# Latent branch: query and key projections as one product of 352 columns, two token blocks at a time, over halves of the rows

## The chip, the cores and the metric

The kernel runs on one core of one Trainium2 chip. The metric is device time of one execution in microseconds (us). The kernel before took 1448.16 us, the median of three runs (1447.72 to 1449.43). A core has a matrix engine (TensorE, PE in the profile), a vector engine (VectorE, DVE), a scalar engine for activations and copies (ScalarE, ACT), a general one (GpSimd, POOL) and a queue that issues transfers (SyncE, SP). Matrix products are written to PSUM, eight banks of 512 fp32 numbers on each of 128 partitions; everything else lives in SBUF.

## The reference

Two layers work on 256 latent tokens (`x`) and 256 context tokens (`ctx`), 1024 channels wide. A layer normalises and modulates the tokens to `h`, projects `h` through `w_in` to the queries, keys and values of four attention branches, gates and merges the branches, and ends with a gated MLP. In layer 1 the context tokens only serve as keys and values: no queries of theirs are needed. The branch that is changed is the fourth, the latent one (MLA):

```python
q = (rms_norm(qa, qa_g) @ w_qb)        # qa: 192 columns of h @ w_in
kv = (rms_norm(kva, kva_g) @ w_kvb)    # kva: 128 columns of h @ w_in
k_rope = rms_norm(kr, ...)             # kr: 32 columns of h @ w_in, shared by the 4 heads
```

Queries and keys get a rotary part of 32 numbers per head (latent tokens only), 4 heads attend over all 512 tokens (context queries over context alone).

## The kernel before

Every large product is made in three matmuls (`mm3`, lines 277 to 280): both factors are split into a high part in the fast fp32 format and a low rest, and high x high, high x low and low x high are added up. The tokens' split halves `hh` and `hl` stay in SBUF, 8 chunks of 128 channels by 512 tokens. A weight tile is loaded and split by `wload` (line 267): one transfer on SP's queue into `raw`, a cast on ACT into `wh` (line 272), a subtraction on DVE into `wl` (line 257, a helper). `raw`, `wh` and `wl` have four slots each, of up to 1024 columns.

`win_block` (line 442) makes one block of columns of `h @ w_in`. It loads two weight tiles (512 rows each) and walks over token halves j (256 tokens) and token blocks a (128 tokens): 8 row chunks times `mm3`, with the tokens as the stationary factor and the weights streaming. Both blocks of a half land in one PSUM buffer of the pool `acc_p` (three buffers, line 243), and a function `use` then takes them out: one copy on ACT, the norm, and a list of later steps. Those wait in the list `later`; `due` runs one of them at each turn of the generator, and `flush` (line 438) runs what is left, one a turn.

For the latent branch there are two such blocks: `mkv` (160 columns: 128 of the key and value rank, 32 rotary; both halves in either layer) with `use_mkv` (line 709), and `mqa` (192 columns; the halves `qh`, both in layer 0 and the first alone in layer 1) with `use_mqa` (line 748). Each leaves five steps per half: a transposition of the normalised rank (`put`), for either token block the second product with `w_kvb` or `w_qb` into an `acc` buffer with its norm and rotary work (`tok`, lines 725 and 764, products at lines 728 and 768), and for either the transposition of the heads into `kT` or `qT` (`mla_T`, line 741).

Several generators are interleaved by `drive` (line 282): each has a weight, and the one whose count of turns divided by its weight is smallest goes next. The drive at lines 1034 to 1037 holds the attention of the third branch (`attend`, weight `na` = 10 per token half), `merge(1, ...)` (line 933, weight 8, one turn per 128 output channels), the chain of the two latent blocks and `flush` (weight 22 in layer 0, 10.64 in layer 1), and in layer 0 four turns of modulation work. A turn of `merge` loads a gate tile, makes the gate product (24 matmuls) into one `acc` buffer, a tanh on ACT (line 943) reads it, makes the branch product (6 matmuls) into another, and a DVE instruction (line 949 or 951, shown under its helper's line 254) reads that. It keeps a branch tile for four turns. The next drive (line 1039) attends over the latent branch and runs `merge(2, ...)`.

The order of this program is the first wish: the kernel is built with `schedule_with_timeline_sim=True`, so a planner that simulates the engines at compile time fixes each engine's order and gives out buffers, and may put a later instruction ahead of one that waits. In the trace the matmuls of different generators do stand mixed.

Of the kernel before, what the change touches and what calls it, by code (L numbers as in the profile page):

```python
# [31 lines left out]
def _r(a, n):  # L32
    return np.arange(a, a + n)
# [4 lines left out]
    "naq": _r(NAQ, 256),  # L38
    "dk": _r(DK, 256), "dv": _r(DV, 256), "dq": _r(DQ, 256),
    "gkv": np.concatenate([_r(GK, 128), _r(GV, 128)]), "gq": GQ_PERM,  # L40
    "mkv": np.concatenate([_r(MKVA, 128), _r(MKR, 32)]), "mqa": _r(MQA, 192),
}
GBR_PERM = np.concatenate([_r(0, 64), _r(128, 64), _r(64, 64), _r(192, 64)])
MOD_GROUPS = [(1, 0), (2, 4), (3, 5)]
FGRP = [(0, 8), (8, 8), (16, 6)]
# [2 lines left out]
def tile_keys():  # L48
    ks = []
    for g in range(3):  # L50
        ks += [("mod", g, kt, half) for kt in range(KD) for half in range(2)]
    ks += [("nakv", t) for t in range(4)]
    ks += [("win", blk, t) for blk in BLOCKS for t in range(2)]
    ks += [("gate", i, m) for i in range(4) for m in range(KD)]
    ks += [("br", i, h) for i in range(4) for h in range(2)]
    ks += [("out", m) for m in range(KD)]
    ks += [("up", f) for f in range(2 * NF)]
    ks += [("down", g, m) for g in range(len(FGRP)) for m in range(KD)]
    ks += [("qb",), ("kvb",)]
    return ks  # L60
# [7 lines left out]
def _kp(w):  # L68

    k, n = w.shape  # L70
    return w.reshape(k // P, P, n).transpose(1, 0, 2).reshape(P, -1)


def host_tile(key, l, w):
    k = key[0]
    if k == "mod":
        _, g, kt, half = key
        if g == 0 and l == 0:
            o = w["w_mod"][0].reshape(2, 4, P, 6, KD, P)[half, :, :, 0:2, kt]
            return o.transpose(1, 0, 2, 3).reshape(P, 1024)  # L80
        c = MOD_GROUPS[g][half] * KD + kt
        return w["w_mod"][l, :, c * P:(c + 1) * P].T
    if k == "nakv":
        return _kp(w["w_in"][l, key[1] * 256:(key[1] + 1) * 256, NAK:NAK + 512])
    if k == "win":
        _, blk, t = key
        return _kp(w["w_in"][l, t * 512:(t + 1) * 512][:, BLOCKS[blk]])
    if k == "gate":
        return _kp(w["w_gate"][l, key[1], :, key[2] * P:(key[2] + 1) * P])
    if k == "br":  # L90
        wb = w["w_branch"][l, key[1]]
        if key[1] == 2:
            wb = wb[GBR_PERM]
        return _kp(wb[:, key[2] * 512:(key[2] + 1) * 512])
    if k == "out":
        return _kp(w["w_out"][l, :, key[1] * P:(key[1] + 1) * P])
    if k == "up":
        return _kp(w["w_up"][l, :, key[1] * P:(key[1] + 1) * P])
    if k == "down":
        f0, n = FGRP[key[1]]  # L100
        return _kp(w["w_down"][l, f0 * P:(f0 + n) * P, key[2] * P:(key[2] + 1) * P])
    if k == "qb":
        a = w["w_mla_qb"][l].reshape(2, 96, 384).transpose(1, 0, 2).reshape(96, 768)
        o = np.zeros((P, 768), a.dtype)
        o[:96] = a
        return o
    if k == "kvb":
        return w["w_mla_kvb"][l]
# [123 lines left out]
def backbone(ctx: ExitStack, tc, wb, xT, cc, cb, sm, rg, bias, cst, out):  # L232
# [209 lines left out]
    def win_block(l, blk, halves, use):  # L442
# [3 lines left out]
        for j in halves:  # L446
# [9 lines left out]
            due(0)  # L456
            yield

    def head_rstd(*parts):

        v = tiny.tile([P, 16], F32, name="v")
        o = 0
        for ap, mul, add in parts:
            a, h, d = ap.shape[1:]
            sq = tmp.tile([P, T], F32, name="t")
            sv = sq[:, :a * h * d].rearrange("p (a h d) -> p a h d", a=a, h=h)
            A.activation(out=sv, in_=ap, func=AF.Square)
            vo = v[:, o:o + a * h]
            V.tensor_reduce(out=vo, in_=sq[:, :a * h * d].rearrange("p (h d) -> p h d", d=d), op=ALU.add, axis=AX.X)
            V.tensor_scalar(out=vo, in0=vo, scalar1=mul, scalar2=add, op0=ALU.mult, op1=ALU.add)  # L470
            o += a * h
        return pow_mhalf(v[:, :o], o)
# [9 lines left out]
    for l in range(L):  # L482
# [225 lines left out]

        def use_mkv(t0, na, ps):
            st = stage()  # L710
            A.copy(st[:, :, 0:160], ps[:, :, 0:160])
            a, krn = st[:, :, 0:128], st[:, :, 128:160]
            r = head_rstd((a.unsqueeze(2), 1.0 / 128, EPS), (krn.unsqueeze(2), 1.0 / 32, EPS))
            tt(V, a, a, r[:, 0:2].unsqueeze(2).to_broadcast([P, 2, 128]), ALU.mult)
            tt(V, krn, krn, r[:, 2:4].unsqueeze(2).to_broadcast([P, 2, 32]), ALU.mult)
            if t0 < 2:
                rope(st[:, :, 160:192].unsqueeze(2), krn.unsqueeze(2), 1, 2, t0)
                krn = st[:, :, 160:192]
            got = {}

            def put():
                got["ma"] = mw["ka"]
                to_T(got["ma"].unsqueeze(1), st[:, :, 0:128], vec("kvag"), A)

            def tok(t):
                ma = got["ma"]
                kv = acc_p.tile([P, 512], F32, name="acc")
                mm(kv, lhsT=ma[:, t * P:(t + 1) * P], rhs=mw["kv"], start=True, stop=True)  # L728
                kv4 = kv.rearrange("p (h d) -> p h d", h=4)
                A.copy(Vt["ml"][:, t0 + t].rearrange("p (h d) -> p h d", h=4), kv4[:, :, 64:128])  # L730
                skv = stage().rearrange("p a n -> p (a n)")[:, :384].rearrange("p (h d) -> p h d", h=4)
                kn = skv[:, :, 0:64]
                A.copy(kn, kv4[:, :, 0:64])
                r = head_rstd((kn.unsqueeze(1), 1.0 / 64, EPS))
                tt(V, kn, kn, r.unsqueeze(2).to_broadcast([P, 4, 64]), ALU.mult)
                G.tensor_copy(skv[:, :, 64:96], krn[:, t].unsqueeze(1).to_broadcast([P, 4, 32]))
                got[t] = lambda: mla_T(kT, skv, t0 + t, vec("mkc" if t0 else "mkx", 0, 96), A)

            return [put, lambda: tok(0), lambda: tok(1), lambda: got[0](), lambda: got[1]()]
# [7 lines left out]

        def use_mqa(t0, na, ps):
            st = stage()
            A.copy(st[:, :, 0:192], ps[:, :, 0:192])  # L750
            r = head_rstd((st[:, :, 0:192].unsqueeze(2), 1.0 / 192, EPS))
            tt(V, st[:, :, 0:192], st[:, :, 0:192], r.unsqueeze(2).to_broadcast([P, 2, 192]), ALU.mult)
            got = {}

            def put():
                tp = tp_p.tile([P, 4, P], F32, name="tp")
                for i in range(2):
                    for a in range(2):
                        nc.tensor.transpose(tp[:96, 2 * i + a], st[:, a, 96 * i:96 * i + 96], ident)
                got["ma"] = mw["qa"]  # L760
                for i in range(2):
                    A.mul(got["ma"][:96, i], tp[:96, 2 * i:2 * i + 2].rearrange("p a t -> p (a t)"), vec("qag", i, 96))

            def tok(t):
                ma = got["ma"]
                qps = acc_p.tile([P, 512], F32, name="acc")
                for i in range(2):
                    mm(qps[:, :384], lhsT=ma[:96, i, t * P:(t + 1) * P], rhs=mw["q"][:96, i], start=i == 0, stop=i == 1)  # L768
                sq_ = stage().rearrange("p a n -> p (a n)")
                A.copy(sq_[:, :384], qps[:, :384])  # L770
                sqv = sq_[:, :384].rearrange("p (h d) -> p h d", h=4)
                q4 = sqv
                r = head_rstd((q4[:, :, 0:64].unsqueeze(1), 1.5, 96 * EPS), (q4[:, :, 64:96].unsqueeze(1), 3.0, 96 * EPS))
                tt(V, sqv[:, :, 0:64], q4[:, :, 0:64], r[:, 0:4].unsqueeze(2).to_broadcast([P, 4, 64]), ALU.mult)
                rr = r[:, 4:8].unsqueeze(2).to_broadcast([P, 4, 32])
                if t0 < 2:
                    qr = sq_[:, 384:512].rearrange("p (h d) -> p h d", h=4)
                    tt(V, qr, q4[:, :, 64:96], rr, ALU.mult)
                    rope(sqv[:, :, 64:96].unsqueeze(1), qr.unsqueeze(1), 0, 2, t0 + t)
                else:  # L780
                    tt(V, sqv[:, :, 64:96], q4[:, :, 64:96], rr, ALU.mult)
                got[t] = lambda: mla_T(qT, sqv, t0 + t, vec("mqc" if t0 else "mqx", 0, 96), V)

            return [put, lambda: tok(0), lambda: tok(1), lambda: got[0](), lambda: got[1]()]
# [222 lines left out]
        for t in range(4):  # L1007
# [25 lines left out]
        O = newO()  # L1033
        drive((attend([(0, 2), (1, 3)], probs_gq, Vt["gq"], lambda h: 64 * (h // 2), post_plain(O)), na),
              (merge(1, O1), 8),
              (chain(win_block(l, "mkv", A2, use_mkv), win_block(l, "mqa", qh, use_mqa), flush()), (16 + nq) * (1, 0.56)[l]),
              *early(4))
        O1 = newO()
        drive((attend(PAIR, probs_ml, Vt["ml"], lambda h: 64 * h, post_plain(O1)), na), (merge(2, O), 8 * (1, 1.96)[l]),
# [187 lines left out]
```

## Time and profile before

| | |
|---|---|
| median of three runs | 1448.16 us |
| profiled execution: its time | 1449.59 us |
| profiled execution: span from first to last instruction | 1447.8 us |
| mean granted TensorE clock | 0.992 of full speed |
| matmuls | 8562 |
| bytes moved by transfers | 202.20 MB |

The profile is of one execution. Busy time of an engine counts its instructions from start to end, and matmuls overlap one another, so for PE the distance from the start of a matmul to the start of the next says what it costs. The chain of waits goes back from the last instruction, at each step to what released it. In layer 0 the matmuls of the two latent blocks run between 250 and 324 us of the span, in layer 1 between 1068 and 1125 us.

### The profile page before, as it was taken

To read this page: it belongs to the slowest core of one execution; us is meant where nothing else is said; L and a number is where in the kernel's file an instruction comes from. 1 tells how busy PE (TensorE), PEld (TensorE's weight loads), DVE (VectorE), ACT (ScalarE), POOL (GpSimd) and SP (SyncE) were. 2 spreads that over 40 slices of the span, in tenths; PEclk is the share of its full clock that TensorE was granted. 3 is DMA by queue.
4 is the path that set the end of the run, shared out by engine and by line. 5 is a ranking of instruction groups with operands and counts; after the bars stand their busy time and mean duration, and the time that the engine had idled before them with its cause. 6 is when DMAs were issued, how large, how long until landed. Compare 5 with 4: busy or idle time off the path is not lost.

```text
span 1447.8 us, 22404 instructions
## 1 busy us (share of the span) xinstructions
PE 1406.1 (97%) x8562; PEld 1194.4 (82%) x8562; DVE 1057.1 (73%) x1976; ACT 656.6 (45%) x1201; POOL 148.4 (10%) x143
## 2 busy tenths in 40 slices
PE   6899999999999999999999999999999999899998
PEld 3687778776777889888888888898898889799998
DVE  5578777657676656999999654777876676686884
ACT  5344555443333334533234432455655554564662
POOL 0243102112100000000000000053122300000000
PEclk9999999999999999999999999999999999899999
DMA  9433032223234441565797222242232334455553
GB/s 376 172 102 95 31 105 79 90 63 128 88 116 161 140 166 45 182 196 177 237 323 238 101 99 84 88 138 89 83 127 96 119 129 133 152 182 185 180 185 107
DMA packets 57931, 202.20 MB, mean 140 GB/s; under 512 B 6560, under 2 KB 8096, under 8 KB 57184
## 3 DMA queue, kind: packets, MB, share of 16 engines
q1 hardware_dynamic: 57824, 200.77, 41.6%
q8 instruction: 68, 1.11, 0.3%
q14 instruction: 39, 0.32, 0.1%
HBM read 199.69 MB, written 1.05 MB: 139 GB/s over the span
## 4 chain that ended last, share of the span: by engine, by line
PE 87%; issue 7%; DVE 3%; ACT 2%; POOL 1%; DMA 1%; SPq 0%; POOLq 0%; DVEq 0%; ACTq 0%
PE acc L278 25%; PE acc L279 24%; PE acc L280 24%; PE av L876 3%; PE sc L792 2%; PE tp L868 2%; DVE wl L257 1%; PE tp L647 1%; PE tp L372 1%; ACT wh L272 1%; PE sc L804 1%; DMA mraw<-in_wb_dram 1%; PE acc L768 1%; PE acc L728 1%; POOL st L257 0%
## 5 line engine op out<-in xcount | busy, mean ns | idle before, releaser
L272 ACT CAST wh<-raw 128x1024 fp32r<-128x1024 f32 (+1 forms) x272 | 279.7, 1029 | 463.3 <-PE acc L279 384.0
L278 PE MATMUL acc<-hh,wh 128*128 128x256 f32 (+1 forms) x1248 | 422.4, 340 | 6.2 <-ACT hh L424 3.9
L257 DVE TENSOR_TENSOR wl<-raw,wh 128x1024 fp32r<-128x1024 f32 (+1 forms) x272 | 326.8, 1202 | 137.1 <-ACT wh L272 135.9
L280 PE MATMUL acc<-hh,wl 128*128 128x256 f32 (+1 forms) x1248 | 419.3, 336 | 0.0
L279 PE MATMUL acc<-hl,wh 128*128 128x256 f32 (+1 forms) x1248 | 418.2, 336 | 0.0
L278 PEld LDWEIGHTS acc<-hh,wh 128*128 128x128 f32 x1248 | 238.5, 192 | 35.1 <-ACT hh L424 4.4
L280 PEld LDWEIGHTS acc<-hh,wl 128*128 128x128 f32 x1248 | 239.0, 192 | 25.1 <-issue 2.8
L279 PEld LDWEIGHTS acc<-hl,wh 128*128 128x128 f32 x1248 | 239.2, 192 | 24.8 <-issue 2.7
L350 DVE SCALAR_TENSOR_TENSOR junk<-raw,cact 128x1024 bf16<-128x1024 f32 x128 | 157.1, 1227 | 17.4 <-DMA raw<-in_wb_dram 17.0
L278 PE MATMUL acc<-wh,hh 128*128 128x256 f32 (+3 forms) x496 | 149.4, 301 | 5.8 <-ACT hh L424 5.8
L257 POOL TENSOR_TENSOR r<-v,mhalf 128x4 f32<-128x4 f32 (+3 forms) x59 | 80.0, 1359 | 701.6 <-DVE v L405 365.1
L279 PE MATMUL acc<-wl,hh 128*128 128x256 f32 (+3 forms) x496 | 147.5, 297 | 0.0
L280 PE MATMUL acc<-wh,hl 128*128 128x256 f32 (+3 forms) x496 | 145.3, 298 | 1.1 <-DVE hl L254 1.1
L279 PE MATMUL acc<-al,wh 128*128 128x256 f32 (+1 forms) x370 | 121.6, 329 | 0.0
L280 PE MATMUL acc<-ah,wl 128*128 128x256 f32 (+1 forms) x370 | 121.6, 329 | 0.0
L278 PE MATMUL acc<-ah,wh 128*128 128x256 f32 (+1 forms) x370 | 121.5, 328 | 0.0
L254 DVE SCALAR_TENSOR_TENSOR u<-acc,smt,u 128x255 f32<-128x255 f32 (+1 forms) x184 | 108.9, 594 | 1.5 <-ACT u L1126 0.4
L278 PEld LDWEIGHTS acc<-wh,hh 128*128 128x128 f32 x496 | 95.4, 192 | 14.6 <-ACT hh L424 8.3
L818 ACT ACTIVATE p<-sc,nm 128x512 f32<-128x512 f32 (+1 forms) x120 | 74.3, 620 | 70.3 <-DVE nm L815 35.2
L280 PEld LDWEIGHTS acc<-wh,hl 128*128 128x128 f32 x496 | 94.9, 192 | 8.9 <-issue 3.4
L279 PEld LDWEIGHTS acc<-wl,hh 128*128 128x128 f32 x496 | 95.5, 193 | 6.7 <-issue 4.2
L815 DVE TENSOR_REDUCE nm<-sc 128x1 f32<-128x512 f32 (+1 forms) x120 | 70.4, 595 | 17.1 <-PE sc L804 7.9
(173 smaller groups left out, 2016.0 us busy)
## 6 DMA issues: line engine op xcount, KB each, us to landing
raw<-in_wb_dram SPq DMA_DIRECT2D x328, 512.0 KB, 3.5
mraw<-in_wb_dram SPq DMA_DIRECT2D x16, 512.0 KB, 10.2
raw<-in_wb_dram SPq DMA_DIRECT2D x20, 384.0 KB, 2.9
x<-in_xT_dram SPq DMA_DIRECT2D x2, 1024.0 KB, 6.3
bt<-in_bias_dram SPq DMA_DIRECT2D x8, 256.0 KB, 2.7
xt<-in_xT_dram SPq DMA_DIRECT2D x2, 1024.0 KB, 8.5
raw<-in_wb_dram SPq DMA_DIRECT2D x4, 320.0 KB, 2.9
cact<-in_cb_dram SPq DMA_DIRECT2D x1, 1024.0 KB, 11.4
```

Of the source, the lines that this page charges most:

```text
L254: return V.scalar_tensor_tensor(out=out, in0=in0, scalar=scalar, in1=in1, op0=op0, op1=op1)
L257: e.tensor_tensor(out=out, in0=a, in1=b, op=op)
L272: A.copy(h[:, :w], r[:, :w])
L278: mm(ps, lhsT=a[0], rhs=b[0], start=first, stop=False)
L279: mm(ps, lhsT=a[0], rhs=b[1], start=False, stop=False)
L280: mm(ps, lhsT=a[1], rhs=b[0], start=False, stop=last)
L350: V.scalar_tensor_tensor(out=junk, in0=r, scalar=1.0, in1=cact[:, st_], op0=ALU.mult, op1=ALU.mult, accum_out=o)
L792: mm(sps[:, :n], lhsT=q[o:o + d, c:c + P], rhs=k[o:o + d, T - n:], start=True, stop=True)
L815: V.tensor_reduce(out=nm, in_=sps[:, :n], op=ALU.max, axis=AX.X, negate=True)
L818: A.activation(out=p[:, :n], in_=sps[:, :n], func=AF.Exp, bias=nm, accum_out=s)
L868: nc.tensor.transpose(tp[:, i], p[:, i * P:(i + 1) * P], ident)
L876: mm(av[64 * j:64 * j + 64], lhsT=V_[:, 4 - nk + i, vcol(hd):vcol(hd) + 64], rhs=PTs[j][:, i], start=i == 0, stop=i == nk - 1, tile_positi ...
```

## The change

A new generator `win_mla` takes the place of the two `win_block`s in the chain. Key and query columns lie side by side in new weight tiles (`("mla", t)`, four per layer, 256 rows by 352 columns). For a half of the tokens it opens two `acc` buffers, one per token block, loads the two tiles of one half of the rows, runs both token blocks over these 4 row chunks, then the other half of the rows. The second half of the tokens begins with the half of the rows that is still loaded, and loads the first one again: six loads a layer in place of four. Where a half needs no queries (layer 1, context), the matmuls take only the first 160 columns. Then both `use` functions run on the two buffers, with one copy per token block, and their ten steps go to `later`, keys first. The weight of the chain in `drive` stays as it was.

```diff
-    "mkv": np.concatenate([_r(MKVA, 128), _r(MKR, 32)]), "mqa": _r(MQA, 192),
 }
+MLA_COLS = np.concatenate([_r(MKVA, 128), _r(MKR, 32), _r(MQA, 192)])
...
+    ks += [("mla", t) for t in range(4)]
...
+    if k == "mla":
+        return _kp(w["w_in"][l, key[1] * 256:(key[1] + 1) * 256][:, MLA_COLS])
...
+    def win_mla(l, halves, use_kv, use_q):
+        n = len(MLA_COLS)
+        for j in range(2):
+            nn = n if j in halves else 160
+            pss = [acc_p.tile([P, T], F32, name="acc") for _ in range(2)]
+            for step, i in enumerate(((0, 1), (1, 0))[j]):
+                if j == 0 or step:
+                    w = [wload(l, ("mla", 2 * i + t), 2, n) for t in range(2)]
+                for a in range(2):
+                    t = 2 * j + a
+                    for kt in range(4):
+                        mm3(pss[a][:, :nn], tuple(z[:, 4 * i + kt, t * P:(t + 1) * P] for z in (hh, hl)),
+                            tuple(z[:, kt % 2, :nn] for z in w[kt // 2]), step == 0 and kt == 0, step == 1 and kt == 3)
+                    due(0)
+                    yield
+            steps = use_kv(2 * j, 2, pss)
+            if j in halves:
+                steps = steps + use_q(2 * j, 2, pss)
+            later.extend([f, 0] for f in steps)
+            due(0)
+            yield
...
         def use_mkv(t0, na, ps):
             st = stage()
-            A.copy(st[:, :, 0:160], ps[:, :, 0:160])
+            for i in range(2):
+                A.copy(st[:, i, 0:160], ps[i][:, 0:160])
...
         def use_mqa(t0, na, ps):
             st = stage()
-            A.copy(st[:, :, 0:192], ps[:, :, 0:192])
+            for i in range(2):
+                A.copy(st[:, i, 0:192], ps[i][:, 160:352])
...
-              (chain(win_block(l, "mkv", A2, use_mkv), win_block(l, "mqa", qh, use_mqa), flush()), (16 + nq) * (1, 0.56)[l]),
+              (chain(win_mla(l, qh, use_mkv, use_mqa), flush()), (16 + nq) * (1, 0.56)[l]),
```

## Rows read from the trace of the kernel before

**Rows 1.** The page: busy time, share of the span and instructions of each engine.

```profile
PE 1406.1 (97%) x8562; PEld 1194.4 (82%) x8562; DVE 1057.1 (73%) x1976; ACT 656.6 (45%) x1201; POOL 148.4 (10%) x143
```

**Rows 2.** The page: busy tenths and granted clock in 40 slices.

```profile
PE   6899999999999999999999999999999999899998
PEclk9999999999999999999999999999999999899999
```

**Rows 3.** The page: the chain of waits, by engine and by line.

```profile
PE 87%; issue 7%; DVE 3%; ACT 2%; POOL 1%; DMA 1%; SPq 0%; POOLq 0%; DVEq 0%; ACTq 0%
PE acc L278 25%; PE acc L279 24%; PE acc L280 24%; PE av L876 3%; PE sc L792 2%; PE tp L868 2%; DVE wl L257 1%; PE tp L647 1%; PE tp L372 1%; ACT wh L272 1%; PE sc L804 1%; DMA mraw<-in_wb_dram 1%; PE acc L768 1%; PE acc L728 1%; POOL st L257 0%
```

**Rows 4.** Windows: stretch, its length, busy us (instructions) per engine, clock, DMA.

```profile
250.00:346.00 96.00, 94.85 (x521) 71.50 (x520) 64.60 (x145) 43.31 (x104) 13.45 (x18) 1.00 0.29 93
1068.00:1146.00 78.00, 76.00 (x554) 64.19 (x553) 50.88 (x108) 43.54 (x92) 17.95 (x21) 1.00 0.34 112
```

**Rows 5.** Groups by line and shape: PE, one of three matmuls of either block.

```profile
L280 PE MATMUL acc<-wh,hl 128*128 128x160 f32 x64 | 17.7, 276 | 0.0
L280 PE MATMUL acc<-wh,hl 128*128 128x192 f32 x48 | 13.2, 274 | 0.0
```

**Rows 6.** Timeline of PE (start, duration): first and last of unbroken stretches.

```profile
269.71 0.28 PE L279 MATMUL acc<-wl,hh 128*128 128x160 f32 x1
...
274.85 0.27 PE L280 MATMUL acc<-wh,hl 128*128 128x160 f32 x1
...
303.94 0.27 PE L279 MATMUL acc<-wl,hh 128*128 128x192 f32 x1
...
306.40 0.28 PE L280 MATMUL acc<-wh,hl 128*128 128x192 f32 x1
...
1088.29 0.28 PE L278 MATMUL acc<-hh,wh 128*128 128x256 f32 x1
...
1090.68 0.28 PE L280 MATMUL acc<-hh,wl 128*128 128x256 f32 x1
...
282.44 0.40 PE L279 MATMUL acc<-hl,wh 128*128 128x512 f32 x1
...
287.49 0.39 PE L280 MATMUL acc<-hh,wl 128*128 128x512 f32 x1
```

**Rows 7.** Groups by line and shape: splitting a 768-column weight tile.

```profile
L272 ACT CAST wh<-raw 128x768 fp32r<-128x768 f32 x20 | 16.7, 835 | 46.7 <-PE acc L279 44.4 <-PE acc L280 2.3
L257 DVE TENSOR_TENSOR wl<-raw,wh 128x768 fp32r<-128x768 f32 x20 | 19.0, 952 | 2.3 <-ACT wh L272 2.3
```

**Rows 8.** Timeline of ACT, DVE, PE in layer 0: handover to the query tiles.

```profile
273.82 0.83 ACT L272 CAST wh<-raw 128x768 fp32r<-128x768 f32 x1 [1.76 <-PE acc L280]
275.16 0.83 ACT L272 CAST wh<-raw 128x768 fp32r<-128x768 f32 x1 [0.51 <-PE acc L280]
...
275.18 0.95 DVE L257 TENSOR_TENSOR wl<-raw,wh 128x768 fp32r<-128x768 f32 x1
...
276.85 0.94 DVE L257 TENSOR_TENSOR wl<-raw,wh 128x768 fp32r<-128x768 f32 x1
...
276.68 0.49 PE L278 MATMUL acc<-Oh,wh 128*128 128x512 f32 x1
277.23 0.44 PE L603 MATMUL tp<-C,st 128*128 128x128 f32 x2
277.91 0.70 PE L792 MATMUL sc<-kA,qA 64*128 64x256 f32 x2 [0.24 <-ACT p L818]
```

**Rows 9.** Timeline of PE, ACT, DVE: readers of a gate and branch product.

```profile
288.88 0.40 PE L280 MATMUL acc<-Oh,wl 128*128 128x512 f32 x1
...
288.64 0.59 ACT L943 ACTIVATE t<-acc 128x512 f32<-128x512 f32 x1
...
289.91 0.68 DVE L254 SCALAR_TENSOR_TENSOR t<-t,acc 128x512 f32<-128x512 f32 x1
```

**Rows 10.** Timeline of PE, layer 1: query product behind its operand's copy.

```profile
1141.39 1.56 PE L768 MATMUL acc<-kB 96*128 96x384 f32 x4 [0.84 <-ACT kB L762]
```

## The prediction, before the changed kernel was run

> **What bounds the kernel now.** First the share of the span that each engine is busy: TensorE (PE) 97%, with VectorE (DVE) and ScalarE (ACT) far below it [rows 1]. Busy matmuls overlap, so this alone does not prove a bound. Second the slices of the span: PE stands at 9 almost throughout, and so does the granted clock, that is, its 2.4 GHz level [rows 2]. Third the chain of waits: PE holds 87% of it, and the three matmul lines of `mm3` hold 74% [rows 3]. Fourth the two stretches in which the changed blocks run, about 250 to 346 us in layer 0 and 1068 to 1146 us in layer 1: PE is busy 94.85 of 96 us and 76.00 of 78 us at clock 1.00, DVE 64.60 and 50.88, ACT 43.31 and 43.54, POOL 13.45 and 17.95 [rows 4]. So matmul time that goes here should come off the span, provided that PE still finds its next matmul ready.
>
> **1. The matmuls.** `win_block` multiplies every block of 128 tokens by 160 key columns and, on its own, by 192 query columns: 8 chunks of rows by 3 matmuls each. Layer 0 has 4 token blocks for either, 96 + 96 matmuls; layer 1 needs queries for 2 blocks, 96 + 48. The trace has 192 matmuls of 160 columns and 144 of 192 (one of three equal groups for each is shown, x64 and x48) [rows 5]. What counts is the distance from start to start, since a mean duration overlaps the next one. Over 47 unbroken matmuls of 160 columns it is (274.85 - 269.71) / 46 = 0.112 us; over 23 of 192 columns, (306.40 - 303.94) / 22 = 0.112; over 21 of 256, (1090.68 - 1088.29) / 20 = 0.1195; over 23 of 512, (287.49 - 282.44) / 22 = 0.2295 [rows 6]. The narrow ones cost alike: 160 and 192 columns lie on a floor, so two separate narrow products pay for it twice. No matmul of 352 columns of this kind is in the trace; its bounds are the rows of 256 and 512. Between these a column costs (0.2295 - 0.1195) / 256 = 0.00043 us, so I take 0.1195 + 96 x 0.00043 = 0.161 us.
>
> Layer 0: 192 x 0.112 = 21.5 us go, 96 x 0.161 = 15.5 come: -6.0. Layer 1: 144 x 0.112 = 16.1 go; 48 x 0.161 + 48 x 0.112 (the second half keeps 160 columns) = 13.1 come: -3.0. Sum **-9.0 us**. With 0.1195 for the new matmul it would be -15.0, with 0.2295 it would be +0.8.
>
> A rule speaks against this. The Trainium skill, page "TensorE: Matmul & The Clock Gate", section "Back-to-back issue gap", gives for the isolated gap of a warm matmul N/2.4 + 2.5 ns. By it 160, 192 and 352 columns are estimated at 69, 82 and 149 ns, and all the change would save about 0.4 us, since the columns in total do not change. The trace does not agree for the narrow ones: 0.112 us for both of them. The same section says that in a stream of weight loads and matmuls both set the spacing, which fits the floor.
>
> **2. The weight tiles.** Before, a layer loads 4 tiles here (2 of 640 columns, 2 of 768); after, 6 of 704, since the first half of the rows is loaded again for the second pair of token blocks. Each load costs a cast on ACT and a subtraction on DVE; the nearest, of 768 columns, take 0.835 and 0.952 us [rows 7]. Two more per layer are 1.7 us on ACT and 1.9 on DVE, in stretches where ACT has 53 and 34 us to spare and DVE 31 and 27 [rows 4]: they are hidden by PE's own work. SP gets two more transfers per layer in its order ahead of later gate weights; the DMA engines are busy 0.29 and 0.34 of these stretches [rows 4], so I cost that at nothing; if the cover goes, what is late is the next gate weight.
>
> What isn't free is the handover from one pair of tiles to the next. Four slots hold split weights; merge keeps two (its branch tile and a gate tile), so the next pair can be cast only when the old pair is done. In layer 0 the pair for the queries is cast from 273.82 on and ready at 277.79; in that time PE did other work, with gaps: a 512-column matmul at 276.68 was followed only 0.55 us later (0.32 more than its 0.23), the two transposes after it by the scores 0.68 later with 0.24 of idleness [rows 8]; that is 0.6 us lost, which I round up to 1.0 for what a row does not show. I count 0 for layer 1's handover, whose PE rows show no such gap, so half a microsecond on average. Each layer has one handover more than before: +1.0 for both layers if each of the four new ones costs 0.5 and the two old ones go. Bounds: 0, and 4 x 4 = 16 if none of the 4 us were covered.
>
> **3. The accumulators.** Three PSUM buffers are shared by the projections, merge (one for the gate product, one for the branch product, in turn) and the steps that follow on keys and queries. Before, a projection held one and left two. After, it holds two from the first matmul of a pass to the copies behind its last, so everybody else has one, for the 10 turns of `win_mla` in its chain: with the steps that `flush` has left, the chain has 10 + 14 = 24 turns in layer 0 (12 + 10 = 22 before) and 10 + 9 = 19 in layer 1 (9 + 8 = 17 before). With one buffer merge can't begin the branch product until the gate product has been read, nor the next gate product until the branch product has been. How late that is: a gate product's last matmul starts at 287.49 and ends about 0.39 us later, [rows 6]; its tanh ends at 289.23, because a cast stands ahead of it on ACT: 1.4 us. The branch product's last matmul ends at 289.28, its reader on DVE at 290.59: 1.3 us [rows 9]. About 2.7 us per step of merge, in which PE must have something else. If the turns run as the weights of `drive` say, 8 x 10/24 = 3.3 steps of merge fall into the passes in layer 0 and 8 x 10/10.64 = 7.5 in layer 1: 11 x 2.7 = 29 us to be covered. To cover it there are the 28.6 us of the projection's own matmuls (15.5 + 13.1), which need no new buffer, the scores, transposes and value products, and whatever later work the planned order pulls forward. I take 7% uncovered, **+2 us**; bounds 0 and +29. Queued behind a waiting gate matmul on PE is everything that PE does, so an uncovered wait goes straight to the span.
>
> **4. Copies and order.** One copy out of PSUM for two token blocks becomes two. ACT pays some 0.3 us more per pass, of its spare time. The steps on the first half's queries, with their rotary work on POOL, now come ahead of the second half's keys, and POOL is busy for 14 and 23% of the two stretches [rows 4]: nothing. Layer 1's last steps are then those of keys without rotary work in place of queries; the 0.84 us that PE waits there for the copy of the normalised queries [rows 10] may go or be replaced by a wait for the keys' copy. I count 0, bounds -1 and +2.
>
> **Sum.** -9.0 + 1.0 + 2.0 = -6.0 us on the profiled execution. That one took 1449.6 us, 1.8 more than its span, and 1.4 more than the median of the runs, 1448.16. So 1448.2 - 6.0 = **1442.2 us**.
>
> **The rivals.**
> *Accumulator starvation (slower).* The one buffer left decides once more than (9.0 - 1.0) / 29 = 28% of the merge waits have no cover. For it: layer 1, where passes fill nearly the whole stage and a step of merge has only 30 x 0.1195 = 3.6 us of matmuls against 2.7 us of waits. Against: matmuls of several generators already stand mixed in PE's order, and 47 matmuls of the key block ran in one go from 269.71 to 274.85 [rows 6], so the projection can fill a wait of several us. At half uncovered: -9.0 + 1.0 + 14.5 = +6.5, 1454.7 us. Chance 0.17.
> *Cost goes by columns (no change).* The columns are the same, 192 x 160 + 144 x 192 = 58368 before and 144 x 352 + 48 x 160 = 58368 after; at the 512-column row's price per column both are 26.2 us. Then 0 + 1.0 + 2.0 = +3.0, 1451.2; without the waits 1448.2. The floor of [rows 6] speaks against it. Chance 0.04. The isolated-gap formula of the Trainium skill's page named above would give this.
> *The gain is given back in handovers and a new order.* Handovers at 1.5 us each instead of 0.5 (four: 6 us) less the old 1.0, and 3 us at the buffers: -9.0 + 5.0 + 3.0 = -1.0, 1447.2. Chance 0.19.
>
> **How the numbers follow.** The forecast holds 0.60; its own range is 1438 to 1446. About 0.2%, 2.9 us, is what a measurement of this kernel tells from no change. Faster: nearly all of the forecast and a little of the third rival, 0.62. Same: most of the third and some of the second, 0.20. Slower: starvation and the rest, 0.18. The range reaches from 1436 (a 352-column matmul at 0.14 us, 144 x 0.021 = 3.0 us less, and no wait added) to 1452 (some 40% of the waits at the buffers uncovered).
>
> **What would show it.** Right: 144 matmuls of 352 columns and 48 of 160, the former some 0.16 us apart; PE busy in both stretches as before, with the stages some 6 and 3 us shorter. Step 2 is wrong if PE idles ahead of 352-column matmuls with a cast or subtraction as what ended it; step 3 if it idles ahead of gate or branch matmuls with tanh or the merge's DVE product as releaser. The prediction is wrong as a whole if the 352-column matmuls stand 0.2 us apart or more, or if the gain of these stages is lost in the next one, with keys or queries of the latent branch coming later than its first scores.

## The result, and the profile after

The changed kernel takes 1456.28 us (median of five runs, 1455.73 to 1457.91); the kernel before, in runs beside it on the same chip, 1449.34. The ratio is 1.0053, with a 95% interval of 1.0043 to 1.0064: it is slower, by 0.53% (the ratios here and below are of all runs, and can differ a little from those of the medians). The prediction, 1442.2 us and a range up to 1452, was wrong in sign. The profiled execution took 1456.99 us, with a span of 1454.8 and a mean granted clock of 0.988.

The page of the changed kernel: busy times, the slices of PE, the chain by engine.

```profile
PE 1402.2 (96%) x8418; PEld 1187.8 (82%) x8418; DVE 1064.4 (73%) x1980; ACT 663.2 (46%) x1212; POOL 149.6 (10%) x143
PE   6899999999999999999999999999989899899999
PE 84%; issue 8%; DVE 4%; ACT 2%; POOL 1%; DMA 1%; SPq 0%; POOLq 0%; DVEq 0%; ACTq 0%
```

There are 144 matmuls fewer, and PE's busy time falls by 3.9 us [rows 1], while the span grows by 7.0. So PE stands idle for longer, and the chain agrees: PE's share falls from 87% to 84%, DVE's and issue's rise by a point each [rows 3]. The slices already show where: 30 and 32 of 40, about 1055 to 1091 and 1127 to 1164 us, were at 9 [rows 2] and are at 8.

First the layers, by marks that both traces have. The first latent matmul of layer 1 starts at 1064.20; before it was at 1068 [rows 4]. Layer 0 thus kept a gain of 3.8 us. From that mark to the end of the span it takes 1454.8 - 1064.2 = 390.6 us, against 1447.8 - 1068.0 = 379.8: layer 1 lost 10.8.

The windows after: layer 1's stretch and two short parts of it (columns as in [rows 4]).

```profile
1064.00:1165.00 101.00, 90.13 (x589) 74.48 (x588) 64.25 (x137) 51.68 (x111) 25.24 (x31) 0.93 0.32 105
1076.90:1083.70 6.80, 5.97 (x20) 4.73 (x17) 3.19 (x6) 4.37 (x8) 1.02 (x1) 0.50 0.00 0
1145.10:1152.00 6.90, 5.95 (x15) 3.09 (x15) 1.77 (x5) 1.54 (x4) 1.55 (x5) 0.51 0.00 0
```

In layer 1's stretch PE is idle for 101.00 - 90.13 = 10.9 us, and the granted clock is 0.93 on average, because for two short parts it is 0.50, the 1.2 GHz level. Before, PE was idle there for 2 us and the clock was 1.00 [rows 4].

What PE waited for from 1064 to 1170 us (us in total, times, longest), and PE's own timeline around it, with two places in layer 0 ahead. In this kernel's numbering L281 to L283 are `mm3`, L641 transposes the third branch's queries and L616 copies them out, L772 transposes the heads of latent keys or queries, L756 makes the keys' second product and L972 is merge's tanh. A matmul of `mm3` that reads `wh,hh` or `wl,hh` or `wh,hl` is a projection's, one that reads `hh,wh` or `hl,wh` or `hh,wl` is merge's gate product.

```profile
PE tp L772 <- POOL st L260: 5.2, 1, 5.2
PE tp L641 <- POOL st L260: 2.4, 1, 2.4
PE av L905 <- DVE PT L620: 0.9, 1, 0.9
PE sc L838 <- ACT qA L616: 0.8, 1, 0.8
PE acc L283 <- DVE wl L260: 0.8, 1, 0.8
PE acc L756 <- ACT kB L618: 0.6, 1, 0.6
```

```profile
269.48 0.43 PE L281 MATMUL acc<-wh,hh 128*128 128x352 f32 x1 [0.96 <-ACT t L972]
...
291.21 0.32 PE L282 MATMUL acc<-wl,hh 128*128 128x352 f32 x1
...
292.82 0.32 PE L283 MATMUL acc<-wh,hl 128*128 128x352 f32 x1
...
1070.44 0.28 PE L283 MATMUL acc<-hh,wl 128*128 128x256 f32 x1
...
1072.01 1.94 PE L905 MATMUL av<-PT,Vt 128*64 128x256 f32 x14 [0.85 <-DVE PT L620]
1076.37 0.68 PE L641 MATMUL tp<-C,st 128*128 128x128 f32 x4 [2.42 <-POOL st L260]
...
1078.31 1.22 PE L838 MATMUL sc<-kA,qA 128*128 128x512 f32 x2 [0.83 <-ACT qA L616]
1079.33 0.49 PE L281 MATMUL acc<-wh,hh 128*128 128x352 f32 x1
...
1082.56 0.49 PE L283 MATMUL acc<-wh,hl 128*128 128x352 f32 x1
...
1104.56 0.38 PE L283 MATMUL acc<-hh,wl 128*128 128x256 f32 x1 [0.76 <-DVE wl L260]
...
1145.37 2.30 PE L772 MATMUL tp<-C,st 128*96 128x128 f32 x8 [5.19 <-POOL st L260]
...
1151.53 0.89 PE L281 MATMUL acc<-hh,wh 128*128 128x256 f32 x1
```

The waits add up to 10.7 us; the kernel before had 1.4 of note there (0.57, and the 0.84 of [rows 10]). All but the last two lines of the list come in two places, which I call the first and the second stop.

The first stop is 1071 to 1078 us. Three waits, 0.85 + 2.42 + 0.83 = 4.1 us, for the copy of a softmax's transposed weights (`PT`), for POOL's rotary work on the third branch's queries, and for the copy behind it. Then the second token block of the new product starts, at 1079.33.

The second stop is at 1140: 5.19 us ahead of the transposition of the latent queries' heads. POOL begins those queries' norm only at 1140.02 and ends their rotary work some 6.5 us later. The timeline of ACT, DVE and POOL in the changed kernel, with merge's readers at the first stop ahead:

```profile
1077.09 1.17 ACT L616 CAST qA<-tp 64x512 fp32r<-64x512 f32 x2 [2.73 <-PE tp L641]
...
1078.56 0.38 ACT L972 ACTIVATE t<-acc 128x256 f32<-128x256 f32 x1
...
1090.42 0.42 DVE L257 SCALAR_TENSOR_TENSOR t<-t,acc 128x256 f32<-128x256 f32 x1 [1.36 <-PE acc L283]
...
1137.71 1.22 DVE L260 TENSOR_TENSOR wl<-raw,wh 128x1024 fp32r<-128x1024 f32 x1
...
1138.35 0.48 ACT L799 COPY st<-acc 128x384 f32<-128x384 f32 x1 [0.16 <-PE acc L797]
...
1140.02 3.24 POOL L260 TENSOR_TENSOR r<-v,mhalf 128x8 f32<-128x8 f32 x2 [3.00 <-DVE v L497]
...
1146.07 0.45 POOL L260 TENSOR_TENSOR st<-st,rb 128x128 f32<-128x128 f32 x1
```

The half clock starts during the first stop, at 1076.9, ahead of its third wait, and at the end of the second, at 1145.1; each time it lasts 6.8 us. Leaving out the idle time that shows inside them (0.83 and 0.95 us), half of 5.97 and of 5.95 busy us, some 3 us each, is the most it can cost. Sum for layer 1: stops +9.3, clock up to +6, matmuls -3.0 by the prediction, that is at most +12.3 where +10.8 was measured.

### The profile page after: what moved, and what is told of

It is laid out like the page before. It is cut to its first block, busy times and chain, and to the rows that moved or that the text cites. A ratio compares the mean times of both kernels' runs of the same rounds, so it can differ in the third digit from the quotient of the medians.

```text
span 1454.8 us, 22144 instructions
## 1 busy us (share of the span) xinstructions
PE 1402.2 (96%) x8418; PEld 1187.8 (82%) x8418; DVE 1064.4 (73%) x1980; ACT 663.2 (46%) x1212; POOL 149.6 (10%) x143
## 4 chain that ended last, share of the span: by engine, by line
PE 84%; issue 8%; DVE 4%; ACT 2%; POOL 1%; DMA 1%; SPq 0%; POOLq 0%; DVEq 0%; ACTq 0%
PE acc L281 24%; PE acc L282 24%; PE acc L283 24%; PE av L905 3%; PE sc L821 2%; PE tp L897 2%; DVE wl L260 1%; POOL r L260 1%; ACT wh L275 1%; PE tp L674 1%; PE sc L833 1%; DMA mraw<-in_wb_dram 1%; PE acc L756 1%; PE tp L375 0%; PE sc L839 0%
## 5 line engine op out<-in xcount | busy, mean ns | idle before, releaser
L275 ACT CAST wh<-raw 128x1024 fp32r<-128x1024 f32 (+2 forms) x276 | 282.8, 1026 | 437.2 <-PE acc L282 358.9
L281 PE MATMUL acc<-hh,wh 128*128 128x256 f32 (+1 forms) x1248 | 421.1, 339 | 6.8 <-ACT hh L427 3.9
L260 DVE TENSOR_TENSOR wl<-raw,wh 128x1024 fp32r<-128x1024 f32 (+2 forms) x276 | 331.2, 1201 | 129.5 <-ACT wh L275 128.0
L283 PE MATMUL acc<-hh,wl 128*128 128x256 f32 (+1 forms) x1248 | 417.1, 335 | 0.8 <-DVE wl L260 0.8
L281 PEld LDWEIGHTS acc<-hh,wh 128*128 128x128 f32 x1248 | 237.9, 191 | 35.6 <-ACT hh L427 4.4
L283 PEld LDWEIGHTS acc<-hh,wl 128*128 128x128 f32 x1248 | 238.2, 191 | 24.7 <-issue 1.8
L260 POOL TENSOR_TENSOR r<-v,mhalf 128x4 f32<-128x4 f32 (+3 forms) x59 | 81.6, 1387 | 705.5 <-DVE v L408 367.7
L281 PE MATMUL acc<-wh,hh 128*128 128x256 f32 (+3 forms) x448 | 139.9, 314 | 6.8 <-ACT hh L427 5.8
L282 PE MATMUL acc<-wl,hh 128*128 128x256 f32 (+3 forms) x448 | 137.8, 308 | 0.0
L283 PE MATMUL acc<-wh,hl 128*128 128x256 f32 (+3 forms) x448 | 135.5, 308 | 1.1 <-DVE hl L257 1.1
L281 PE MATMUL acc<-ah,wh 128*128 128x256 f32 (+1 forms) x370 | 121.5, 328 | 0.0
L283 PE MATMUL acc<-ah,wl 128*128 128x256 f32 (+1 forms) x370 | 121.4, 328 | 0.0
L281 PEld LDWEIGHTS acc<-wh,hh 128*128 128x128 f32 x448 | 86.5, 193 | 17.6 <-ACT hh L427 8.3
L283 PEld LDWEIGHTS acc<-wh,hl 128*128 128x128 f32 x448 | 86.0, 193 | 8.8 <-issue 3.4
L282 PEld LDWEIGHTS acc<-wl,hh 128*128 128x128 f32 x448 | 86.9, 194 | 7.6 <-issue 3.5
L844 DVE TENSOR_REDUCE nm<-sc 128x1 f32<-128x512 f32 (+1 forms) x120 | 70.6, 597 | 20.1 <-PE sc L833 10.7
```

The lines of the kernel that those rows point to most:

```text
L260: e.tensor_tensor(out=out, in0=a, in1=b, op=op)
L275: A.copy(h[:, :w], r[:, :w])
L281: mm(ps, lhsT=a[0], rhs=b[0], start=first, stop=False)
L282: mm(ps, lhsT=a[0], rhs=b[1], start=False, stop=False)
L283: mm(ps, lhsT=a[1], rhs=b[0], start=False, stop=last)
L844: V.tensor_reduce(out=nm, in_=sps[:, :n], op=ALU.max, axis=AX.X, negate=True)
```

## The experiments

The theory after the result: the narrow matmuls were saved as forecast, and layer 1 loses more than that at the two stops, each of which is a long chain on other engines (norm, rotary work, transposition, copy) that PE no longer has matmuls to cover. The second stop is due to the order of the steps, the first to accumulators and halved rows. The rivals: layer 1 loses it in general, over all merge steps, or the new weight tiles cost it.

**l0_only.** Layer 1 has its old blocks back (with their weight tiles and copies), layer 0 keeps the new product.

```diff
...
-              (chain(win_mla(l, qh, use_mkv, use_mqa), flush()), ...
+              (chain(*([win_block(l, "mkv", A2, use_mkv), win_block(l, "mqa", qh, use_mqa)] if l else
+                       [win_mla(l, qh, use_mkv, use_mqa)]), flush()), ...
```

> The new product in layer 0 alone; layer 1 keeps the two separate blocks. Theory: the loss lies wholly in layer 1's stage, where PE stops twice behind POOL's rotary work and then runs at half clock, while layer 0 keeps its gain of about 5 us: 1449.3 - 5 = 1444 us. Rival: the two-buffer passes cost something everywhere and the early 5 us of layer 0 are given back later whatever layer 1 does: 1449 to 1451 us.

Measured: 1444.96 us against 1449.19 before, ratio 0.9973 (0.9962 to 0.9985), faster. The whole loss is layer 1's: 1456.28 - 1444.96 = 11.3 us, and layer 0 alone is worth 4.2. The window of layer 1's stretch in this kernel has no low clock and 2.0 us of idle PE:

```profile
1062.00:1160.00 98.00, 96.00 (x712) 83.18 (x711) 66.55 (x139) 54.18 (x112) 26.33 (x31) 1.00 0.35 115
```

**kv_first.** In layer 1 the steps of the queries go behind those of the second half's keys, the order that the kernel before had.

```diff
-                steps = steps + use_q(2 * j, 2, pss)
+                qs_ = use_q(2 * j, 2, pss)
+                if l == 0:
+                    steps = steps + qs_
+            if l and j:
+                steps = steps + qs_
```

> The changed kernel, but in layer 1 the five steps of the queries run after those of the second half's keys instead of before them. Theory: the stop of 5.2 us at 1140 comes from the order: behind the queries' transpositions, which wait for POOL's rotary work, stand the keys' two second products, and behind these the accumulators of the next merge, which are handed out in the order of the program. With queries last, the next merge can run in the meantime: the 5.2 us and most of the 3.4 us that the half clock after it costs go, 1456.3 - 8.6 = 1448 us; the stop at 1074 stays. Rival: the stop comes from the chain being two turns longer at the same weight, so that more of its steps run alone; that is not changed here, and the time stays at 1455 to 1457 us.

Measured: 1455.41, ratio 1.0040 (1.0028 to 1.0053). The order of the steps by itself is not the cause; that part of the theory fell. PE's timeline shows the 5.19 us gone and two other waits, 3.67 us together, in its place, at the same time of the stage (L634 transposes the normalised key rank there, L776 the heads):

```profile
1136.48 0.41 PE L634 MATMUL tp<-C,st 128*128 128x128 f32 x2 [2.33 <-DVE st L260]
...
1144.30 1.05 PE L776 MATMUL tp<-C,st 128*96 128x128 f32 x8 [1.34 <-DVE st L260]
```

Whichever chain stands first, nothing fills the wait for it. That is odd, since the next drive's `merge(2, ...)` has matmuls that need nothing from this branch. They need an accumulator, though. In the changed kernel the accumulators stood empty: the last product before the second stop was copied out by 1138.83 (L799), and merge's next weights were split by 1138.93 (DVE's L260), while the gate product starts at 1151.53. So neither room nor weights were missing. In the order of the built programs, before and after, the three `acc` buffers are first used in the order in which the program opens them (the only exceptions after are the second buffers of the pairs). The keys' second products (L756) open theirs ahead of merge's next step, so merge queues behind them, and they behind the stopped chain.

**kv_in_sc.** To test that, layer 1's second products of the context keys take a buffer of the scores' pool, and all else stays as changed.

```diff
-                kv = acc_p.tile([P, 512], F32, name="acc")
+                kv = sc_p.tile([P, 512], F32, name="sc") if l and t0 else acc_p.tile([P, 512], F32, name="acc")
```

> The changed kernel with its order of steps as it is, but in layer 1 the second products of the context tokens' keys are written to a buffer of the scores' pool and not to an accumulator. Theory: the next merge's accumulators no longer queue behind these products, its matmuls fill the wait for POOL, and the stop of 5.2 us at 1140 goes with the half clock after it: about 1448 us. Rival: the transpositions are first in PE's order simply because they are first in the program, whatever buffers are free; the stop stays, 1455 to 1457 us.

Measured: 1450.05, ratio 1.0005 (0.9996 to 1.0014), 6.2 us less than the changed kernel. PE's timeline:

```profile
1136.74 0.58 PE L281 MATMUL acc<-hh,wh 128*128 128x256 f32 x1
...
1144.95 0.28 PE L281 MATMUL acc<-hh,wh 128*128 128x256 f32 x1
1145.54 0.60 PE L772 MATMUL tp<-C,st 128*96 128x128 f32 x4
...
1146.91 0.64 PE L772 MATMUL tp<-C,st 128*96 128x128 f32 x4 [0.76 <-POOL st L260]
```

The chain of the queries is as late as in the changed kernel (1145.54 against 1145.37), but merge's products, with one of the attention between them, now run from 1136.74 to 1145 in front of it, and 0.76 of the 5.19 us is left. The half clock behind it is gone too. So the second stop is the accumulators' order, shown. A new wait of 1.6 us, of a merge product for an accumulator that tanh had yet to read, takes back some; the first stop stands as it was.

**ctx_first.** Now the first stop. In layer 1 the context half runs first, as a block of 160 columns in one accumulator with whole 512-row tiles; the latent half follows with 352 columns.

```diff
...
-        for j in range(2):
+        for j in range(2) if l == 0 else halves:
...
-              (chain(win_mla(...), flush()), ...
+              (chain(*([win_block(l, "mkv", [1], use_mkv)] if l else []), win_mla(...), flush()), ...
```

> The changed kernel, but in layer 1 the context half of the keys runs first, as a block of 160 columns in one accumulator with weight tiles of its own (two of 640 columns), and then the latent half as 352 columns in two accumulators; queries' steps are last by that. Theory: the stop of 2.4 us at 1074 with the two short ones beside it and the half clock after it (some 7 us) comes from the second accumulator that the first pass wants while merge holds the other two; with one accumulator there are 48 matmuls to run in that wait, so both stops go, and what is left is the gain on the matmuls: 1456.3 - 8.6 - 7 = 1441 us. Rival: the first stop has another cause (the weight tiles' handover, or POOL's rotary work coming late): it stays, 1447 to 1449 us.

Measured: 1449.59, ratio 1.0004 (0.9996 to 1.0013): 6.7 us less than the changed kernel, and not the full gain. The first stop fell from 4.1 us to one wait of 1.49, with no low clock behind it. Yet later in the stage one of the second kind came up, at the latent keys' norm, and the clock stood at 0.50 from 1119.9 to 1126.7:

```profile
1122.12 0.66 PE L631 MATMUL tp<-C,st 128*128 128x128 f32 x2 [4.47 <-DVE st L261]
```

**two_buffers.** The reverse: the kernel before, with its 160-column key block of layer 1 in two accumulators, one per token block; rows not halved.

```diff
-            ps = acc_p.tile([P, 2, 256], F32, name="acc")
+            if two:
+                ps = [acc_p.tile([P, T], F32, name="acc") for _ in range(2)]
...
```

> The kernel before with one thing of the change: in layer 1 the 160-column key block of a token half takes two accumulators, one per token block, in place of one, with one copy per block. Theory: the second accumulator is what opens the stop at the start of layer 1's stage, because merge holds the other two; some 24 matmuls fewer stand ready during POOL's rotary work, PE stops there by 2 to 4 us, with or without a half clock after it: 1449.2 + 3 to 7 = 1452 to 1456 us. Rival: the stop in the changed kernel came from other weight tiles and their handover: no stop here, 1449 to 1450 us.

Measured: 1449.91 against 1448.66, ratio 1.0006 (0.9998 to 1.0015): no difference, where several us of loss were expected. The second accumulator alone isn't the first stop. PE's timeline shows 0.78 us of wait for `PT` and 0.66 for an accumulator, 1.4 in all; then the second token block's 24 matmuls run while POOL ends its work on the queries, so that their transposition (L617) does not wait. What releases the second block is L716, the copy of the first block's result: over whole rows the first block is finished with 24 matmuls and hands its own accumulator on.

```profile
1075.70 1.94 PE L883 MATMUL av<-PT,Vt 128*64 128x256 f32 x14 [0.78 <-DVE PT L596]
...
1078.30 0.34 PE L278 MATMUL acc<-wh,hh 128*128 128x160 f32 x1 [0.66 <-ACT st L716]
...
1081.05 0.61 PE L617 MATMUL tp<-C,st 128*128 128x128 f32 x4
```

**ctx_first_sc** and its control **l0_only_sc.** ctx_first and l0_only, each with all second products of layer 1, keys' and queries', in the scores' pool.

```diff
...
-                qps = acc_p.tile([P, 512], F32, name="acc")
+                qps = sc_p.tile([P, 512], F32, name="sc") if l else acc_p.tile([P, 512], F32, name="acc")
```

> The version with the context half first, and in layer 1 the second products of keys and queries go to the scores' pool. Theory: its stop of 4.5 us at 1118 is PE waiting for the norm of the latent keys while merge's next gate product queues for an accumulator behind the keys' second products; with these in another pool the gate product moves ahead: 1449.6 - 4.5 - 3 (half clock) = 1442 us. Rival: what is missing there is work that the separate query product used to supply, and no buffer changes it: the stop stays or turns up elsewhere, 1447 to 1450 us.

> The version with the new product in layer 0 alone, and in layer 1 the second products of keys and queries in the scores' pool: the control for the run beside it. Theory: layer 1 with its separate blocks has no stop beyond 0.9 us, so the pool gives at most about 1 us: 1444 to 1445 us. Rival: the pool by itself is worth several us, and then it says nothing of the new product: 1441 us or less.

Measured: ctx_first_sc 1444.85 against 1448.66, ratio 0.9974 (0.9965 to 0.9982), faster. l0_only_sc 1448.79, ratio 1.0000 (0.9991 to 1.0009): 3.8 us slower than l0_only, which was not expected. PE's waits in ctx_first_sc: the stop of 4.47 is down to 0.5, and a wait for tanh is there.

```profile
PE acc L282 <- ACT t L976: 1.9, 1, 1.9
...
PE tp L631 <- DVE st L261: 0.5, 1, 0.5
```

The control has that wait too, here in the timeline of ACT and PE:

```profile
1145.49 0.48 ACT L806 COPY st<-sc 128x384 f32<-128x384 f32 x1 [1.05 <-PE sc L804]
...
1146.52 0.46 ACT L806 COPY st<-sc 128x384 f32<-128x384 f32 x1
...
1147.53 0.77 ACT L979 ACTIVATE t<-acc 128x256 f32<-128x256 f32 x2
...
1147.95 0.38 PE L282 MATMUL acc<-Oh,wh 128*128 128x256 f32 x1 [1.91 <-ACT t L979]
```

Merge's tanh stands behind the copies of both query products on ACT, and PE waits 1.91 us for the accumulator that it reads; 3.4 us at clock 0.50 follow. So the scores' pool is no free place either. With equal pools the new product in layer 1 comes out 1448.79 - 1444.85 = 3.9 us ahead, but that is no measure of the 3.0 that its matmuls should save: the 3.4 us at half clock, up to 1.7 us, stand in the control's profile alone, although ctx_first_sc has the same wait of 1.91.

**ctx_first_kvsc.** ctx_first with only the latent keys' second products in the scores' pool.

```diff
...
-                kv = acc_p.tile([P, 512], F32, name="acc")
+                kv = sc_p.tile([P, 512], F32, name="sc") if l and not t0 else acc_p.tile([P, 512], F32, name="acc")
```

> The version with the context half first, and in layer 1 only the latent keys' two second products in the scores' pool; those of the queries stay in accumulators. Theory: the stop of 4.5 us at 1118 goes as it did with all of them moved, since it was these two that stood between the gate product and its accumulator, and the wait of 1.9 us at 1145, which the control shows as well, comes from the queries' products in the scores' pool and goes too: 1444.9 - 2 = 1443 us, and under the version with the new product in layer 0 alone (1445). Rival: the queries' products are what held up merge, so the stop of 4.5 us stays: 1448 to 1450 us.

Measured: 1445.78 against 1448.69, ratio 0.9968 (0.9957 to 0.9980). The wait at the keys' norm is no longer among PE's waits, as expected, nor is the one for tanh, but a wait for `PT` grew from 1.3 us in ctx_first to 2.1, with 3.4 us at clock 0.50 behind it. How far the gain falls short of the expected 1443 is not settled: the runs reach from 1442.04 to 1446.90, and the profile is of the slowest.

```profile
PE av L909 <- DVE PT L621: 2.1, 1, 2.1
```

**row_halves.** The first stop without the wide product: the kernel before, whose key block of layer 1 runs as the change has it, in two accumulators over halves of the rows (256-row tiles of 160 columns, six loads); the query block is as before.

```diff
...
-    return _kp(w["w_in"][l, key[1] * 256:(key[1] + 1) * 256][:, MLA_COLS])
+    return _kp(w["w_in"][l, key[1] * 256:(key[1] + 1) * 256][:, MLA_COLS[:160]])
...
+              (chain(win_mla(l, [], use_mkv, None) if l else win_block(l, "mkv", A2, use_mkv),
+                     win_block(l, "mqa", qh, use_mqa), flush()), ...
```

> The kernel before, but in layer 1 the 160-column key block runs in the changed kernel's manner: two accumulators per token half, one per token block, and halves of the rows (256-row tiles of 160 columns, six loads), so that just 12 matmuls stand on the first accumulator before the second is needed; the query block is separate as before. Theory: with 12 in place of 24 ready matmuls the stop at the start of layer 1's stage grows from the 1.4 us of the two-accumulator run to the 4.1 us of the changed kernel, and a half clock follows: 1448.7 + 4 to 7 = 1453 to 1456 us. Rival: the halves of the rows do nothing of the kind and it is the queries' steps that come with the product: 1449 to 1450 us, as with two accumulators alone.

Measured: 1465.34 against 1449.03, ratio 1.0116 (1.0099 to 1.0133), far more than was expected. PE's timeline and a window:

```profile
1067.57 0.24 PE L282 MATMUL acc<-wh,hh 128*128 128x160 f32 x1
...
1068.77 0.28 PE L284 MATMUL acc<-wh,hl 128*128 128x160 f32 x1
...
1075.62 1.94 PE L908 MATMUL av<-PT,Vt 128*64 128x256 f32 x14 [1.01 <-DVE PT L621]
1079.98 0.66 PE L642 MATMUL tp<-C,st 128*128 128x128 f32 x4 [2.42 <-POOL st L261]
...
1081.89 1.22 PE L841 MATMUL sc<-kA,qA 128*128 128x512 f32 x2 [1.04 <-ACT qA L617]
1083.05 0.42 PE L283 MATMUL acc<-wl,hh 128*128 128x160 f32 x1
...
1085.18 0.41 PE L284 MATMUL acc<-wh,hl 128*128 128x160 f32 x1
```

```profile
1081.80:1098.80 17.00, 16.91 (x64) 14.13 (x65) 8.38 (x20) 7.34 (x19) 1.02 (x1) 0.50 0.19 63
```

The first stop is here as in the changed kernel, wait for wait: 1.01 + 2.42 + 1.04 = 4.5 us against 4.1. Only 12 matmuls run ahead of it, and the second token block's come behind it. So it needs neither the 352 columns nor the fused steps; halved rows with an accumulator per token block make it, and the same two accumulators with whole rows (two_buffers) don't. The extra loads are not it: in this stage PE waits for a split weight once, 0.22 us, ahead of merge's gate product. Its price is larger here because 17.0 us at the lower clock follow, at most 8.5 us of cost, and later waits of 1.7 and 1.6 us.

The mechanism of the first stop, read from these rows: a token block over half the rows has 4 x 3 = 12 matmuls. Then it isn't finished and keeps its accumulator, and the next 12 need another. In the changed kernel the two others are held by merge. Its branch product is read only at 1090.42, so the buffer that the second block gets at 1079.33 is the gate product's, free when tanh ends at 1078.94 (in the built program, too, the second block has the gate product's bank). And tanh is late by order, not by work: the gate product's last matmul starts at 1070.44, but on ACT tanh stands behind the copies (L616) of the very queries that PE waits for. So the matmuls that could cover this wait are held up by it themselves. Before, all 48 matmuls of a token half, 160 columns each, went into one buffer, and all of them stood between 1068 and 1078 us in that place. Whether tanh ahead of these copies would be a cure was not tried, and a fourth accumulator has no room, since all eight banks are in use.

## Why the prediction was wrong, point by point

**Step 1, the matmuls: right.** Ten spacings of 352 columns from 291.21 to 292.82 give (292.82 - 291.21) / 10 = 0.161 us, the interpolated value. The isolated-gap formula of the Trainium skill, page "TensorE: Matmul & The Clock Gate", section "Back-to-back issue gap", gives an estimate of 149 ns here; the trace is 8% above it. The rival that cost goes by columns is out: layer 0 alone gained 4.2 us at equal columns (l0_only).

**Step 2, the weight tiles: about right in size, not in place.** In neither layer does a 352-column matmul wait for a cast or a subtraction, where 1.0 us had been counted for handovers. The one wait on a split weight, 0.76 us at 1104.56 in layer 1, is ahead of merge's gate product (`hh,wl`): the late gate weight that the prediction named and put at nothing.

**Step 3, the accumulators: mis-sized in layer 1.** In layer 0 the two waits of note are 0.96 us for merge's tanh, ahead of a 352-column matmul at 269.48, and 1.01 for a norm; a wait of 0.7 on the scores went. So -6.0 + 2.0 - 0.7 = -4.7, where 4.2 us were gained. For both layers together the prediction held 28.6 us of projection matmuls, "which need no new buffer", against 29 us of waits. In layer 1 that is true of 12 at a time only: the next 12 need a buffer from merge, at the moment when the matmuls were wanted as cover. The two terms of that balance are not independent. The first stop, 4.1 us and up to 3 of clock, is where this shows; without the second stop the changed kernel still stands 1450.05 - 1444.96 = 5.1 us above l0_only.

**Step 4, copies and order of the steps: the step that failed.** It was costed at 0, up to +2, by POOL's busy share. The measured price of the stop that it caused is 6.2 us (kv_in_sc). A share of 23% says that POOL has room, not that its answer comes soon: from the start of the norm to the last rotary result the queries' chain holds POOL for 6.5 us. I named the copy that would be late next, and not the accumulators that the keys' products would hold open behind it, nor that the fused product leaves no projection matmuls for the time of the first norm: before, the query block's matmuls, from 1113 to 1125 us, stood between the copy of the second half's keys (1104.55) and the transposition of their normalised rank (1124.66). kv_first shows that reversing the order doesn't cure it, kv_in_sc that letting merge past does. The two rows of ACT and PE in the kernel before:

```profile
1104.55 0.48 ACT L711 COPY st<-acc 128x320 f32<-128x320 f32 x1
...
1124.66 0.38 PE L603 MATMUL tp<-C,st 128*128 128x128 f32 x2
```

**The clock: not in the sum.** The prediction priced every wait by its length. In layer 1 the granted clock fell to its 1.2 GHz level at two of them, and there 352-column matmuls stand (1082.56 - 1079.33) / 11 = 0.294 us apart. Up to 3 us each time comes on top of waits of 4 to 5 us.

**The rivals.** Starvation came near in number, 1454.7, and named the resource; that the number is near is luck, since it placed the price in even portions at all of merge's steps, 11 x 2.7 us at half cover, and the runs show two places. Handovers are not where the gain went.

**Versions that beat both.** l0_only, 1444.96, ctx_first_sc, 1444.85, and ctx_first_kvsc, 1445.78, tie with each other (their intervals overlap) and are 3 to 4 us faster than the kernel before by their medians; l0_only is the smallest edit. A planner that knows these waits was not tried.

## What to carry to other kernels

When two products are fused, ask what ran on TensorE while the first one's results went through their norm: a second, separate product was cover, and fusing starts both chains at once with nothing behind them. Count an accumulator in ready matmuls: here one that took 48 before the next was needed bridged the wait and one that took 12 didn't, whatever the totals said. Ask also when it comes free: a block that stops half-way keeps its buffer, one that is finished hands it on. And where buffers are handed out in program order, a product that waits for a slow chain blocks everyone behind it in its pool; put it in another pool, or test the change layer by layer and keep the half that gains.

## What the runs showed of the hardware that was not expected

A few us of waiting can cost more than themselves. In the changed kernel the granted clock was 0.50 for 6.8 us after waits of 0.85 and 2.42 us (the one of 0.83 lies in it), and again after one wait of 5.19; in row_halves, after 1.01, 2.42 and 1.04 us, for 17.0 us, although PE was busy for 16.91 of these. There 160 columns stand (1085.18 - 1083.05) / 10 = 0.213 us apart, against 0.112 before [rows 6]. two_buffers, with 1.4 us of waits, and ctx_first's 1.49 us at the first stop kept clock 1.00.

The waits alone don't settle it. Every kernel with the new product in layer 0 has the same wait of 1.01 us there, for a norm at 288 to 289 us; in the profile of ctx_first_kvsc alone the clock falls behind it, for 3.4 us, as this window of it shows:

```profile
289.00:292.50 3.50, 3.50 (x8) 2.46 (x9) 1.46 (x5) 1.53 (x5) 1.43 (x5) 0.51 0.02 5
```

Why like waits are followed by nothing, by 3.4, by 6.8 or by 17.0 us at half clock stays open.
